# A chunked recurrence's block products moved from 128x128 to 64x64 tiles of the TensorE array

## The chip, the cores and the metric

The kernel runs on one core of one Trainium2 chip, as one program. The metric is device time in microseconds (us), the median of several runs. TensorE (PE) multiplies, and its weight loads are listed as an engine of their own (PEld). VectorE is DVE, ScalarE is ACT, GpSimd is POOL, and SyncE (SP) issues the DMAs.

## The reference, cut to what matters

The program computes two model blocks one after the other. The change lies in one mixer of the second block, a delta-rule recurrence over 512 tokens with 16 heads of width 64:

```python
def rwkv7_step(S, inp):
    r_t, dec_t, k_t, v_t, kk_t, a_t = inp
    sa = jnp.einsum('bhij,bhj->bhi', S, -kk_t)
    S = (S * dec_t[:, :, None, :]
         + sa[..., None] * (kk_t * a_t)[:, :, None, :]
         + v_t[..., None] * k_t[:, :, None, :])
    y = jnp.einsum('bhij,bhj->bhi', S, r_t)
    return S, y
...
S0 = jnp.zeros((B, H, N, N), jnp.float32)
_, y = lax.scan(rwkv7_step, S0, seq)
```

The kernel doesn't step token by token. It cuts the 512 tokens into 8 chunks of 64, and inside a chunk it solves the delta rule with the inverse of a 64x64 unit lower triangular matrix I+N, one for each head and chunk.

## The kernel before, in words

Two heads make a pair: head j of a pair lies on partitions 64j to 64j+63 (`hs[j]`). There are eight pairs, and two pairs make a quad. The recurrence is worked off in eight steps g: quad g // 2, and of its eight chunks the four of half g % 2.

`unit` prepares the four chunks of one pair for one g. It computes the inner products of the operands BK and AR (L1571), masks them with DVE into N, ME and RB, and inverts I+N. In bf16 it doubles the size of the inverted blocks over five levels: each level is a product z, a masked copy of it into Z by DVE (L1613), and the products T and Tt, which ACT copies out of PSUM (`keep`, L1606). Two refinements in float32 follow. All of these products come from `prod`: four matmuls, one for each chunk, each 128x128, with the two heads of a pair as the two 64x64 blocks on the diagonal of a 128x128 tile and zeros beside them. `turned` transposes four such tiles (L1601), and L1589 and L1638 transpose operands. `units` runs the generators of the two pairs of a quad step by step in turn.

`chain` is the serial part: 32 times (8 g with 4 chunks) it takes both pairs from the state of one chunk to that of the next. A chunk goes over gp (L1670), G (ACT, L1672), up (L1674), UV (ACT, two copies), xp (L1682) and the next XV (DVE, L1684), and adds two products per head to the output y: from XV (L1694) and from UV (L1695).

The main loop alternates one stage of `chain`, at a raised priority, with two steps of the units in flight (`advance`; STEPS = 24 steps for the 12 stages of a g). A scheduler then orders the instructions of each engine, and each engine runs its own in that order. A float32 product whose operands are not marked fp32r is one instruction in the program and two matmul passes in the trace; a bf16, an fp32r or a transposing one is one pass. Products in bf16 stand in the program as two instructions, LDWEIGHTS and MATMUL.

Before the first chain chunk the V projection (`values`, L366 to L368) fills PE; at the end the output projection does (`output_begin`, L1761).

Of the kernel before, what the change touches and what calls it, by code (L numbers as in the profile page):

```python
# [19 lines left out]
P = 128  # L20
# [1438 lines left out]
def rwkv_core(k, scr, filler, vstack, xsp):  # L1459
# [6 lines left out]
    with ExitStack() as s1, ExitStack() as s2:  # L1466
# [9 lines left out]
        NZ = 4  # L1476
        N_ = [cp.tile([P, 4, P], F32, name=f"N{i}") for i in range(NZ)]
        for n in N_:
            nc.vector.tensor_copy(n, c["ident"].unsqueeze(1).to_broadcast([P, 4, P]))
        Z_ = [[cp.tile([P, 4, P], BF, name=f"Z{l}_{i}") for l in range(5)] for i in range(2)]  # L1480
        for i in range(2):
            for l in range(5):
                nc.gpsimd.tensor_copy(Z_[i][l], c["b_ident"].unsqueeze(1).to_broadcast([P, 4, P]))
        mrw = c["m_rw"]
        bid = c["b_ident"]
        ide = c["ident"]
        two_i = c["two_i"].unsqueeze(1).to_broadcast([P, 4, P])
        one_i = ide.unsqueeze(1).to_broadcast([P, 4, P])
# [60 lines left out]
        count = [0]  # L1549
# [5 lines left out]
        def unit(g, ops, pr):  # L1555

            hf = par = g % 2
            p, AR, BK, bo, pl = ops
            N, Z = N_[count[0] % NZ], Z_[count[0] % 2]
            count[0] += 1  # L1560
            ME = held(g % 3).tile([P, 2, 4, P], F32, name="ME")
            RB = held(g % 3).tile([64, 2, 4, 64], F32, name="RB")
# [4 lines left out]
            for j in range(2):  # L1567
                a = psum()
                for u in range(4):
                    ch = 4 * hf + u  # L1570
                    nc.tensor.matmul(a[:, u], BK[hs[j], ch].rearrange("p a b -> p (a b)"),  # L1571
                                     AR[hs[j], ch].rearrange("p a b -> p (a b)"), start=True, stop=True)
                nc.sync.dma_start(ME[0:64, j], AR[hs[j], 4 * hf:4 * hf + 4].rearrange("p c a b -> p c (a b)"))
                nc.vector.copy_predicated(N[hs[j], :, hs[j]],
                                          mrw[0:64, 0:64].bitcast(I32).unsqueeze(1).to_broadcast([64, 4, 64]),
                                          a[0:64, :, 0:64])
                nc.vector.tensor_tensor(ME[64:P, j], a[64:P], mrw[64:P].unsqueeze(1).to_broadcast([64, 4, P]), op=ALU.mult)
                nc.vector.tensor_tensor(RB[:, j], a[0:64, :, 64:], mrw[0:64, 64:].unsqueeze(1).to_broadcast([64, 4, 64]), op=ALU.mult)
            yield
            Nb = tp.tile([P, 4, P], BF, name=f"Nb{par}")  # L1580
            nc.vector.tensor_scalar(Nb, N, -1.0, None, op0=ALU.mult)

            half = BK[:, 4 * hf:4 * hf + 4]
            nc.gpsimd.tensor_tensor(half.rearrange("p c a b -> p c (a b)"), half.rearrange("p c a b -> p c (a b)"),
                                    pl[:, 4 * hf:4 * hf + 4].unsqueeze(2).to_broadcast([P, 4, P]), op=ALU.mult)
            BT = held(g % 3).tile([P, 4, P], F32, name="BT")
            ps = psum()
            for u in range(4):
                nc.tensor.transpose(ps[:, u], BK[:, 4 * hf + u].rearrange("p a b -> p (a b)"), ide)  # L1589
            nc.scalar.copy(BT, ps)  # L1590
            def prod(lhs, rhs):
                o = psum()
                for u in range(4):
                    nc.tensor.matmul(o[:, u], lhs[:, u] if len(lhs.shape) == 3 else lhs,  # L1594
                                     rhs[:, u] if len(rhs.shape) == 3 else rhs, start=True, stop=True)
                return o

            def turned(t):
                o = psum()
                for u in range(4):  # L1600
                    nc.tensor.transpose(o[:, u], t[:, u].bitcast(F32), ide)  # L1601
                return o

            def keep(o, dt=F32R):
                t = tp.tile([P, 4, P], dt, name=("qr" if dt != BF else "qb") + str(par), bufs=4)
                nc.scalar.copy(t, o)  # L1606
                return t

            T, Tt = bid, bid
            for l in range(5):  # L1610
                yield
                z = prod(Nb, T)
                nc.vector.copy_predicated(Z[l], c[f"lv{l}"].bitcast(I16).unsqueeze(1).to_broadcast([P, 4, P]), z)  # L1613
                yield
                if l == 0:
                    T = Z[0]
                else:
                    T = keep(prod(Tt, Z[l]), F32R if l == 4 else BF)
# [3 lines left out]
            yield  # L1622
            z = prod(N, T.bitcast(F32))
            Z5 = tp.tile([P, 4, P], F32R, name=f"qr{par}", bufs=4)
            nc.vector.tensor_tensor(Z5, two_i, z, op=ALU.subtract)
# [4 lines left out]
            z = prod(N, T.bitcast(F32))  # L1630
            E = tp.tile([P, 4, P], F32R, name=f"qr{par}", bufs=4)
# [277 lines left out]
```

## Time and profile before

| | us |
|---|---|
| median of 3 runs (2564.41 to 2565.99) | 2565.23 |
| the profiled execution | 2561.08 |
| its span, first to last instruction | 2558.9 |
| PE busy in the span | 2437.7 |
| DVE busy | 1544.6 |
| ACT busy | 1096.5 |

The span lies 2.2 us below the time of its own execution, and that lies 4.1 us below the median. A matmul's entry as busy runs to the end of its pipeline, so that PE counts as busy in short gaps between matmuls; how densely matmuls follow each other is read from the length of a run of equal ones. The recurrence lies between about 980 and 1360 us of the span.

### The profile page before, as it was taken

The numbers are of one execution on the slowest core, as the hardware profiler recorded it, in microseconds if no ns is written. First come the engines' busy times: TensorE is split into PE (matmuls) and PEld (weight loads), VectorE is DVE, ScalarE is ACT, GpSimd is POOL, SyncE is SP. The second block draws the span as 40 slices with busy tenths as digits, with TensorE's granted clock in tenths as the row PEclk, the third lists the DMA queues.
The fourth block names the chain that finished last, engine by engine and source line by source line (L and its number), as shares of the span: only waits on it lengthen the run. The fifth ranks groups of instructions, "written<-read, shape, count | busy, mean of one in ns | idle before, by whom it ended". The sixth has DMA issues, their size and how long they took to land.

```text
span 2558.9 us, 32838 instructions
## 1 busy us (share of the span) xinstructions
PE 2437.7 (95%) x13114; PEld 1954.6 (76%) x13114; DVE 1544.6 (60%) x2194; ACT 1096.5 (43%) x1762; POOL 244.5 (10%) x222
## 2 busy tenths in 40 slices
PE   6999999999997999999999899999999798999997
PEld 5777777888886777788877688888865587888886
DVE  5345665633445877777547566565789665656555
ACT  5464544422323444666544443232432443423333
POOL 1001000000000564433101000000000100000000
PEclk8999999999998999999999999999999899999999
DMA  5112335122223335221143122222244131222221
GB/s 174 62 55 77 132 115 180 66 96 99 99 99 132 124 137 205 83 60 54 43 147 138 54 86 95 99 99 99 97 149 137 41 116 50 99 99 99 99 88 61
DMA packets 79126, 258.55 MB, mean 101 GB/s; under 512 B 10361, under 2 KB 21881, under 8 KB 61177
## 3 DMA queue, kind: packets, MB, share of 16 engines
q1 hardware_dynamic: 78972, 256.45, 29.8%
q8 instruction: 103, 1.69, 0.3%
q14 instruction: 51, 0.41, 0.0%
HBM read 217.94 MB, written 25.43 MB: 95 GB/s over the span
## 4 chain that ended last, share of the span: by engine, by line
PE 87%; DVE 5%; DMA 3%; ACT 3%; issue 2%; POOL 0%; SPq 0%; DVEq 0%; ACTq 0%; POOLq 0%
PE ps L366 21%; PE ps L367 21%; PE ps L368 20%; PE pt L1594 3%; PE ps L1203 1%; DVE wlo L331 1%; PE y L1695 1%; PE fl L366 1%; DMA raw<-xkv 1%; PE fl L367 1%; ACT whi L330 1%; PE fl L368 1%; PE pt L1571 1%; PE y L1694 1%; PE o L783 1%
## 5 line engine op out<-in xcount | busy, mean ns | idle before, releaser
L330 ACT CAST whi<-raw 128x2048 fp32r<-128x2048 f32 (+4 forms) x251 | 346.4, 1386 | 567.1 <-PE ps L368 450.8
L331 DVE TENSOR_TENSOR wlo<-raw,whi 128x2048 fp32r<-128x2048 f32 (+4 forms) x238 | 396.7, 1672 | 197.1 <-ACT whi L330 193.0
L937 DVE TENSOR_TENSOR x<-ps,x 128x512 f32<-128x512 f32 x94 | 64.1, 690 | 218.8 <-PE ps L368 218.8
L1127 ACT ACTIVATE cv<-u,vecs 128x512 f32<-128x512 f32 x88 | 63.0, 721 | 150.3 <-DVE u L1125 150.1
L1125 DVE TENSOR_TENSOR u<-ps,rms 128x512 f32<-128x512 f32 x88 | 60.3, 689 | 76.1 <-PE ps L368 76.0
L331 POOL TENSOR_TENSOR wlo<-raw,whi 128x512 fp32r<-128x512 f32 (+2 forms) x13 | 32.1, 2477 | 600.9 <-ACT whi L330 600.9
L1333 POOL TENSOR_SCALAR mx<-h,vecs 128x512 f32<-128x512 f32 x40 | 81.2, 2035 | 62.3 <-DVE mx6l L358 28.1
L1606 ACT CAST qb<-pt 128x512 bf16<-128x512 f32 x112 | 63.8, 590 | 36.1 <-PE pt L1594 35.3
L1128 DVE SCALAR_TENSOR_TENSOR cv<-u,vecs,cv 128x512 f32<-128x512 f32 x88 | 65.7, 749 | 11.2 <-ACT cv L1127 10.9
L366 PE MATMUL ps<-xg0h,wlo 128*128 128x512 f32 x164 | 68.3, 419 | 0.0
L1129 DVE SCALAR_TENSOR_TENSOR cv<-u,vecs,cv 128x512 f32<-128x512 f32 x88 | 65.8, 749 | 1.7
L367 PE MATMUL ps<-xg0l,whi 128*128 128x512 f32 x164 | 64.4, 393 | 1.0 <-DVE xg0l L361 1.0
L1613 DVE CAST_PREDICATED Z<-ball,pt 128x512 bf16<-128x512 int16 x80 | 53.1, 683 | 20.2 <-PE pt L1594 19.7
L367 PE MATMUL ps<-xg6l,whi 128*128 128x512 f32 x164 | 64.0, 390 | 1.1 <-DVE xg6l L361 1.1
L367 PE MATMUL ps<-xg7l,whi 128*128 128x512 f32 x164 | 63.9, 390 | 0.5 <-DVE xg7l L361 0.5
L368 PE MATMUL ps<-xg0h,whi 128*128 128x512 f32 x164 | 64.3, 392 | 0.0
L366 PE MATMUL ps<-xg1h,wlo 128*128 128x512 f32 x164 | 64.2, 392 | 0.0
L367 PE MATMUL ps<-xg1l,whi 128*128 128x512 f32 x164 | 64.2, 392 | 0.0
L368 PE MATMUL ps<-xg1h,whi 128*128 128x512 f32 x164 | 64.2, 392 | 0.0
L366 PE MATMUL ps<-xg2h,wlo 128*128 128x512 f32 x164 | 64.1, 392 | 0.0
L368 PE MATMUL ps<-xg7h,whi 128*128 128x512 f32 x164 | 64.0, 390 | 0.0
L368 PE MATMUL ps<-xg3h,whi 128*128 128x512 f32 x164 | 64.0, 390 | 0.0
(1239 smaller groups left out, 7150.5 us busy)
## 6 DMA issues: line engine op xcount, KB each, us to landing
raw<-ffn_in SPq DMA_DIRECT2D x44, 1024.0 KB, 4.8
raw<-xkv SPq DMA_DIRECT2D x64, 256.0 KB, 3.0
raw<-w_up SPq DMA_DIRECT2D x16, 1024.0 KB, 4.8
raw<-w_down SPq DMA_DIRECT2D x16, 1024.0 KB, 4.7
raw<-ffn_out SPq DMA_DIRECT2D x16, 1024.0 KB, 4.7
rk_scr<-ev SPq DMA_DIRECT2D x48, 256.0 KB, 2.1
ut<-ub SPq DMA_DIRECT2D x128, 67.5 KB, 2.0
raw<-w_in_fm SPq DMA_DIRECT2D x16, 512.0 KB, 3.9
```

Of the source, the lines that this page charges most:

```text
L330: a = hi_on.tensor_copy(hi[:, m], raw) if hi_on else nc.scalar.copy(hi[:, m], raw)
L331: b = (lo_on or nc.vector).tensor_tensor(lo[:, m], raw, hi[:, m].bitcast(F32), op=ALU.subtract)
L366: nc.tensor.matmul(ps, wl, xh, start=start, stop=False, skip_group_check=skip)
L367: nc.tensor.matmul(ps, wh, xl, start=False, stop=False, skip_group_check=skip)
L368: nc.tensor.matmul(ps, wh, xh, start=False, stop=stop, skip_group_check=skip)
L937: nc.vector.tensor_tensor(k.x[i], ps, k.x[i], op=ALU.add)
L1127: nc.scalar.activation(t, u[:, 2:], AF.Copy, scale=d(2))
L1128: nc.vector.scalar_tensor_tensor(t, u[:, 1:S + 1], d(1), t, op0=ALU.mult, op1=ALU.add)
L1129: nc.vector.scalar_tensor_tensor(t, u[:, 0:S], d(0), t, op0=ALU.mult, op1=ALU.add)
L1333: nc.gpsimd.tensor_scalar(t, h[m][:, 0:S], k.v(f"mu{i}", m), None, op0=ALU.mult)
L1594: nc.tensor.matmul(o[:, u], lhs[:, u] if len(lhs.shape) == 3 else lhs, rhs[:, u] if len(rhs.shape) == 3 else rhs, start=True, stop=True)
L1606: nc.scalar.copy(t, o)
```

## The change

Two pairs now share a tile: `unit` handles both pairs of a quad at once, in tiles of shape [128, 2, 4, 64] (pair, chunk, column), with head 0 of each pair on partitions 0 to 63 and head 1 below. No zeros are stored beside the blocks. `prod` issues 16 matmuls of 64x64 instead of four of 128x128 for each pair, with the two heads in turn, which uses two of the four 64x64 tiles of the array: rows 0 to 63 with columns 0 to 63, and rows 64 to 127 with columns 64 to 127. Both write the same PSUM tile, on its two halves of partitions. The inner products use all four 64x64 tiles (x and y). `turned` and the operand transposes become float32 products with a 64x64 identity (`token_major`), and the fp32r tiles become float32. In `chain`, up is split by head, and the product of XV with ME for the output moves ahead to stand right behind gp.

```diff
-        N_ = [cp.tile([P, 4, P], F32, name=f"N{i}") for i in range(NZ)]
-        Z_ = [[cp.tile([P, 4, P], BF, name=f"Z{l}_{i}") for l in range(5)] for i in range(2)]
+        N_ = [cp.tile([P, 2, 4, 64], F32, name=f"N{i}") for i in range(2)]
+        Z_ = [[cp.tile([P, 2, 4, 64], BF, name=f"Z{l}_{i}") for l in range(5)] for i in range(2)]
...
-            for j in range(2):
-                a = psum()
+            for i, (p, AR, BK, bo, pl) in enumerate(both):
...
+                x, y = psum(), psum()
                 for u in range(4):
                     ch = 4 * hf + u
-                    nc.tensor.matmul(a[:, u], BK[hs[j], ch].rearrange("p a b -> p (a b)"),
-                                     AR[hs[j], ch].rearrange("p a b -> p (a b)"), start=True, stop=True)
...
+                    for o, cols, kind in ((x, (0, 1), 0), (y, (1, 0), 1)):
+                        for j in range(2):
+                            nc.tensor.matmul(o[hs[cols[j]], u], BK[hs[j], ch, kind],
+                                             AR[hs[j], ch].rearrange("p a b -> p (a b)"), start=True, stop=True)
...
             def prod(lhs, rhs):
-                o = psum()
-                for u in range(4):
-                    nc.tensor.matmul(o[:, u], lhs[:, u] if len(lhs.shape) == 3 else lhs,
-                                     rhs[:, u] if len(rhs.shape) == 3 else rhs, start=True, stop=True)
+                o = eight(psum())
+                for i in range(2):
+                    for u in range(4):
+                        for r in hs:
+                            nc.tensor.matmul(o[r, i, u], lhs[r, i, u], rhs[r, i, u] if len(rhs.shape) == 4 else rhs[r],
+                                             start=True, stop=True)
                 return o
...
             def turned(t):
-                o = psum()
-                for u in range(4):
-                    nc.tensor.transpose(o[:, u], t[:, u].bitcast(F32), ide)
-                return o
...
+                return prod(t, idc)
...
+            def token_major(src, cols, put):
+
+                os = [eight(psum()) for _ in range(2)]
+                for i in range(2):
+                    for u in range(4):
+                        for j in range(2):
+                            for n, q in enumerate(cols):
+                                nc.tensor.matmul(os[j][hs[q], i, u], src(i, u, n)[hs[j]], idc[hs[j]], start=True, stop=True)
+                for j in range(2):
+                    put(j, os[j])
...
         def chain(hf, us, UV, XV, XN, PL, yps):
...
+                out = lambda pr, j: yps[pr][hs[j], ch * 64:ch * 64 + 64]
+                for pr in range(2):
+                    for j in range(2):
+                        nc.tensor.matmul(out(pr, j), XV[:, u, j, pr], MEs[pr][:, j, u, 64:], start=True, stop=False)
                 G = hA.tile([P, 2, 64], F32, name="G")
                 yield i, nc.scalar.mul(G, gp, -1.0)
                 for pr in range(2):
-                    i = nc.tensor.matmul(up[:, pr], us[pr][3][:, u], G[:, pr], start=True, stop=True)
+                    for j in range(2):
+                        i = nc.tensor.matmul(up[hs[j], pr], T2t[hs[j], pr, u], G[hs[j], pr], start=True, stop=True)
...
                 for pr in range(2):
-                    ME, RB, _, _ = us[pr]
                     for j in range(2):
-                        o = yps[pr][hs[j], ch * 64:ch * 64 + 64]
-                        nc.tensor.matmul(o, XV[:, u, j, pr], ME[:, j, u, 64:], start=True, stop=False)
-                        i = nc.tensor.matmul(o, UV[0:64, u, j, pr], RB[:, j, u], start=False, stop=True)
+                        i = nc.tensor.matmul(out(pr, j), UV[0:64, u, j, pr], RBs[pr][:, j, u], start=False, stop=True)
```

How this moves the instructions on PE is seen at two places; a row is line, operation, written tile, read tiles (moving operand's tile and the weights' tile, in either order), shape of the output, and how many follow each other. The first is the output part of a chunk in `chain`. Before, the products with UV (L1695) and with ME and XV (L1694) take turns, and the next chunk's gp (L1670) comes in between:

```order
L1571 MATMUL pt_11075<-AR,BK 128x128 x4
L1695 MATMUL y<-RB,UV 64x64
L1694 MATMUL y<-ME,XV 64x64
L1695 MATMUL y<-RB,UV 64x64 x2
L1670 MATMUL pc<-XV,ME 64x64
L1694 MATMUL y<-ME,XV 64x64
L1670 MATMUL pc<-XV,ME 64x64
L1695 MATMUL y<-RB,UV 64x64
```

Now gp is L1685, the product with ME and XV is L1689, up is L1694, xp is L1702 and the product with UV is L1712; L1612 is `prod`, L1631 `token_major`, and L1727 and L1733 belong to `post`:

```order
L1685 MATMUL pc<-XV,ME 64x64 x4
L1689 MATMUL y<-ME,XV 64x64 x4
L1631 MATMUL pt_13116<-idc,vv 64x64 x8
L1727 MATMUL ps<-y,call 128x512
L1694 MATMUL pc<-G,T2t 64x64 x4
L1631 MATMUL pt_13117<-idc,vv 64x64 x8
L1612 MATMUL pt_13138<-qr_13084,qr_13103 64x64 x9
L1712 MATMUL y<-RB,UV 64x64
L1702 MATMUL pc<-UV,BT 64x64 x4
L1712 MATMUL y<-RB,UV 64x64 x3
L1612 MATMUL pt_13138<-qr_13084,qr_13103 64x64 x7
```

The four products of a kind now stand together; over the recurrence the places where PE goes from one tile size to another fall from 350 to 222. The second place is in the middle of a unit. Before, PE alternates between the pairs, four matmuls each:

```order
L1594 LDWEIGHTS Nb_11114
L1594 MATMUL pt_11182<-Z_1_7980,Nb_11114 128x128
L1670 MATMUL pc<-XV,ME 64x64
L1694 MATMUL y<-ME,XV 64x64 x2
L1601 MATMUL pt_10902<-r_ident,qr_10877 128x128 x4
L1594 MATMUL pt_10909<-qr_10870,N_7969 128x128 x4
```

Now 16 pairs of LDWEIGHTS and MATMUL of one product (the last pair of one and the first of the next are shown) stand between two stages of the chain:

```order
L1612 LDWEIGHTS Z_1_7995
L1612 MATMUL pt_12797<-qb_12747,Z_1_7995 64x64
L1702 MATMUL pc<-UV,BT 64x64 x4
L1712 MATMUL y<-RB,UV 64x64 x4
L1612 LDWEIGHTS Nb_12674
L1612 MATMUL pt_12827<-qb_12795,Nb_12674 64x64
```

Over the recurrence the bf16 products go from 832 to 1664 and the float32 passes of the units (float32, fp32r and transposes) from 864 to 2816; DVE's masked copies into Z go from 80 to 40, and ACT's copies at `keep` from 176 to 88, each of the same 128x512 elements.

## Rows read from the trace of the kernel before

**Rows 1.** The page's first part: busy us of each engine, share of span, instructions.

```profile
PE 2437.7 (95%) x13114; PEld 1954.6 (76%) x13114; DVE 1544.6 (60%) x2194; ACT 1096.5 (43%) x1762; POOL 244.5 (10%) x222
```

**Rows 2.** Busy time in the stretches of the recurrence, all engines.

```profile
core 0: us, PE busy (x) PEld busy (x) DVE busy (x) ACT busy (x) POOL busy (x), PEclk, DMA share, GB/s
980.00:1016.00 36.00, 32.65 (x140) 24.58 (x138) 26.04 (x42) 14.86 (x22) 5.82 (x12) 0.91 0.59 206
1016.00:1066.00 50.00, 43.65 (x373) 35.15 (x372) 39.12 (x64) 33.87 (x64) 21.15 (x21) 0.97 0.44 136
1066.00:1300.00 234.00, 230.81 (x2361) 191.70 (x2359) 160.13 (x284) 144.67 (x322) 64.36 (x81) 1.00 0.18 51
1300.00:1322.00 22.00, 20.38 (x150) 15.82 (x149) 9.03 (x14) 9.19 (x19) 0.79 (x2) 0.77 0.68 258
```

**Rows 3.** The chain that ended last, by line, 1066 to 1300 us.

```profile
by line: PE pt L1594 32.9%; PE y L1695 10.6%; PE pt L1571 9.7%; PE y L1694 8.5%; PE pt L1601 5.7%; PE pc L1674 4.8%; PE pc L1670 4.6%; PE pc L1682 4.5%; PE pt L1589 2.8%; PE ps L1710 2.6%; PE ps L1716 2.4%; PE ps L1544 1.6%; ACT qb L1606 1.
```

**Rows 4.** The instructions of line L1670 (gp), with first and last start.

```profile
L1670 PE MATMUL pc<-XV,ME x256: 222/222/367, 1066.2 to 1321.8; 128*64 128x64 f32 x128
```

**Rows 5.** PE groups by line, 980 to 1335 us: passes, busy us, mean ns.

```profile
L1695 PE MATMUL y<-RB,UV 64*64 64x64 f32 x256 | 37.1, 243 | 1.6 <-ACT UV L1676 1.6
L1694 PE MATMUL y<-ME,XV 128*64 128x64 f32 x256 | 35.9, 238 | 0.0
L1594 PE MATMUL pt<-qr,N 128*128 128x128 f32 x256 | 35.7, 283 | 0.3 <-ACT qr L1606 0.3
L1571 PE MATMUL pt<-AR,BK 64*128 64x128 f32 x256 | 33.3, 285 | 0.4 <-DVE RB L1578 0.2
L1594 PE MATMUL pt<-Z,qb 128*128 128x128 bf16 x256 | 24.9, 221 | 3.3 <-DVE Z L1613 2.5 <-ACT qb L1606 0.5
L1594 PE MATMUL pt<-qr,qr 128*128 128x128 f32 x128 | 21.5, 290 | 0.5 <-ACT UV L1641 0.4
L1674 PE MATMUL pc<-G,T2t 128*128 128x64 f32 x128 | 19.7, 277 | 0.6 <-ACT G L1672 0.6
L1601 PE MATMUL pt<-r_ident,qr 128*128 128x128 f32 x128 | 19.6, 277 | 0.0
L1589 PE MATMUL pt<-r_ident,BK 128*128 128x128 f32 x64 | 10.1, 280 | 0.8 <-DVE RB L1578 0.4 <-ACT BT L1590 0.2
```

**Rows 6.** PE's timeline at 1168 us: start, length of the run, matmuls.

```profile
1168.04 0.61 PE L1594 MATMUL pt<-qb,Nb 128*128 128x128 bf16 x8
1168.58 0.33 PE L1695 MATMUL y<-RB,UV 64*64 64x64 f32 x2
1168.83 0.33 PE L1694 MATMUL y<-ME,XV 128*64 128x64 f32 x2
1169.09 0.33 PE L1695 MATMUL y<-RB,UV 64*64 64x64 f32 x2
...
1169.46 0.57 PE L1682 MATMUL pc<-UV,BT 128*64 128x64 f32 x7
1169.96 0.44 PE L1695 MATMUL y<-RB,UV 64*64 64x64 f32 x4
```

**Rows 7.** The same view at 1173 and at 1202 us.

```profile
1173.14 0.46 PE L1670 MATMUL pc<-XV,ME 128*64 128x64 f32 x8 [0.23 <-issue]
...
1202.07 0.33 PE L1695 MATMUL y<-RB,UV 64*64 64x64 f32 x4
```

**Rows 8.** The same view at 1181 and at 1206 us.

```profile
1181.28 2.00 PE L1594 MATMUL pt<-qr,N 128*128 128x128 f32 x16
...
1205.99 1.71 PE L1571 MATMUL pt<-AR,BK 64*128 64x128 f32 x16
```

**Rows 9.** DVE and ACT groups by line, 980 to 1335 us, as rows 5.

```profile
L1613 DVE CAST_PREDICATED Z<-ball,pt 128x512 bf16<-128x512 int16 x80 | 53.1, 683 | 20.2 <-PE pt L1594 19.7
...
L1606 ACT CAST qb<-pt 128x512 bf16<-128x512 f32 x112 | 63.8, 590 | 36.1 <-PE pt L1594 35.3
L1606 ACT CAST qr<-pt 128x512 fp32r<-128x512 f32 x64 | 36.5, 590 | 19.5 <-PE pt L1594 11.1 <-PE pt L1601 8.0
```

More of the change, by code (lines that the diff above doesn't have):

```diff
@@ L1553, in held, with unit @@
             return later["h"] if i else hA
-        def unit(g, ops, pr):
+        def unit(g, both):
             hf = par = g % 2
[L1558 to L1562, printed above, removed]
+            N, Z = N_[par], Z_[par]
+            hb = 1 if g % 3 == 0 else 2
+            BT = held(g % 3).tile([P, 2, 4, P], F32, name="BT", bufs=hb)
+            MEs, RBs = [], []
@@ L1596, in prod, with keep @@
                 return o
             def turned(t):
-                o = psum()
-                for u in range(4):
-                    nc.tensor.transpose(o[:, u], t[:, u].bitcast(F32), ide)
-                return o
-            def keep(o, dt=F32R):
-                t = tp.tile([P, 4, P], dt, name=("qr" if dt != BF else "qb") + str(par), bufs=4)
+                return prod(t, idc)
+            def keep(o, dt=F32):
+                t = tp.tile([P, 2, 4, 64], dt, name=("qr" if dt != BF else "qb") + str(par), bufs=4)
@@ L1610, in unit @@
+            T, Tt = None, bic
             for l in range(5):
-                yield
-                z = prod(Nb, T)
-                nc.vector.copy_predicated(Z[l], c[f"lv{l}"].bitcast(I16).unsqueeze(1).to_broadcast([P, 4, P]), z)
+                z = prod(Nb, T if l else bic)
+                nc.vector.copy_predicated(flat(Z[l]), over(lvc[:, l].bitcast(I16)), flat(z))
                 yield
@@ L1616, in unit @@
                     T = Z[0]
+                    token_major(lambda i, u, n: both[i][2][:, 4 * hf + u, n], (0, 1),
+                                lambda j, o: nc.scalar.copy(BT[:, :, :, hs[j]], o))
                 else:
-                    T = keep(prod(Tt, Z[l]), F32R if l == 4 else BF)
+                    T = keep(prod(Tt, Z[l]), F32 if l == 4 else BF)
                 if l == 4:
@@ L1621, in unit @@
                 Tt = keep(turned(T)) if l == 4 else keep(prod(Z[l], Tt), BF)
[L1622 to L1625, printed above, removed]
+                yield
+            z = prod(N, T)
+            Z5 = tp.tile([P, 2, 4, 64], F32, name=f"qr{par}", bufs=4)
+            nc.vector.tensor_tensor(flat(Z5), over(twc), flat(z), op=ALU.subtract)
             yield
@@ L1629, in unit, with place @@
             Tt = keep(turned(T))
[L1630 to L1632 removed]
+            z = prod(N, T)
+            E = tp.tile([P, 2, 4, 64], F32, name=f"qr{par}", bufs=4)
+            nc.vector.tensor_tensor(flat(E), over(idc), flat(z), op=ALU.subtract)
             yield
             UV, XV = values(g)
[L1635 to L1642 removed]
+            vvs = [value(b[0], b[3]) for b in both]
+            def place(j, o):
+                nc.scalar.copy(UV[64:P, :, j], o[64:P].rearrange("p r u d -> p u r d"))
+                nc.gpsimd.tensor_copy(XV[64:P, :, j], UV[64:P, :, j])
+            token_major(lambda i, u, n: vvs[i][:, hf * 256 + u * 64:hf * 256 + u * 64 + 64], (1,), place)
             yield
             z = prod(E, Tt)
[L1645 to L1659 removed]
+            T2t = held(g % 2).tile([P, 2, 4, 64], F32, name="T2t", bufs=1)
+            nc.vector.tensor_tensor(T2t, z, Tt, op=ALU.add)
+            return MEs, RBs, BT, T2t
         def chain(hf, us, UV, XV, XN, PL, yps):
             nonlocal SP
+            MEs, RBs, BT, T2t = us
             for u in range(4):
@@ L1817, in begin @@
                 aside()
-            running.append((g, units(*[(g, quads[g // 2][1][i], i) for i in range(2)])))
+            running.append((g, unit(g, quads[g // 2][1])))
             if g % 2 and g < KT - 1:
```

86 lines of the change are left out of this document (36 added, 50 removed).

## The prediction

> **What bounds the kernel now.** The page gives the whole first: PE is busy in 95% of the span, DVE in 60%, ACT in 43% [rows 1]. That is an average over many stages, so I read the stretches of the recurrence next [rows 2]. From 1066 to 1300 us PE is busy for 230.8 of 234 us, DVE for 160, ACT for 145, at a granted clock of 1.00, which is 2.4 GHz. Before that, from 1016 to 1066, PE is busy for 43.7 of 50 us and DVE for 39; from 1300 on the chain ends and the output projection begins. The chain that ended last goes almost only over PE lines of the units (L1594, L1571, L1601, L1589) and of the chain (L1670 to L1695), and an ACT copy has 1.6% [rows 3]. So PE's own queue sets the pace. The first and last gp show it from the other side: 32 chunks start within 255.6 us [rows 4], 8.2 us for each of the 31 steps.
>
> A busy PE may still be a badly packed one. A run of n equal passes lasts n-1 starts and one pass from its start to its end, so its length gives the time from start to start. Eight bf16 passes with 128 weight columns take 0.61 us, one takes 0.22: (0.61 - 0.22) / 7 = 0.056 us [rows 5, 6]. Sixteen float32 passes on 128 columns: (2.00 - 0.28) / 15 = 0.115 [rows 5, 8]. Float32 passes with 64 columns that stay on one tile: (0.57 - 0.222) / 6 = 0.058 [rows 4, 6]. With 64 columns that alternate between the two column halves of the array (gp): (0.46 - 0.222) / 7 = 0.034, and four 64x64 passes that alternate take 0.33 us where four mostly on one tile take 0.44 [rows 4, 6, 7]: two tiles work at once, and a long run should come near half of 0.058, 0.029. I take **0.030** for 64-column passes that alternate. Two row halves at once show only at the inner products, which write different PSUM tiles: 16 passes in 1.71 us, (1.71 - 0.285) / 15 = 0.095 against 0.115 [rows 5, 8], a partial overlap where j goes from 0 to 1.
>
> Going from one tile size to another has a price. L1695 (64 rows) and L1694 (128 rows) start 0.255 us apart with two passes each [rows 6]; two passes should take 0.116, so a change costs 0.14 us.
>
> **The change, part by part** (passes counted in the order, prices as above, us over the whole recurrence).
>
> Chain. *up*: 128 passes x 0.115 = 14.7 become 256 x 0.030 = 7.7, so -7.0. *Output*: 512 passes x 0.058 = 29.7. The half with ME now alternates, 256 x 0.030 = 7.7; the half with RB keeps its tile from one to the next about every second time, 256 x 0.044 = 11.3; together -10.7. *Changes of tile size*: 350 become 222, 128 x 0.14 = -17.9. gp and xp are as before. Sum of the chain: **-35.6**.
>
> Units. *bf16*: 832 x 0.056 = 46.6 become 1664 x 0.030 = 49.9, +3.3. Half the zeros are gone, but a pass does a quarter of the array and twice as many are needed. *Float32 products, fp32r and transposes*: (256 + 128 + 128) x 0.115 = 58.9 become 1536 x 0.030 = 46.1, -12.8. *Inner products*: 256 x 0.095 = 24.3. The new ones have 64 weight columns but stream 128 columns, for which there is no row; 512 passes cost between 512 x 0.115 / 4 = 14.7 (four tiles at once) and 512 x 0.115 / 2 = 29.4 (two). I take 20, nearer to four, since x and y are separate PSUM tiles: -4. *Transposes of operands*: 96 x 0.115 = 11.0 become 768 x 0.030 = 23.0, +12. Sum of the units: **-1.5**.
>
> PE in all: -37. DVE and ACT lose half of the Z copies, 40 x 0.683 = 27.3 us, and half of `keep`, 88 x 0.59 = 51.9 us [rows 9]. Between 1066 and 1300 neither engine is the bound, so I cost this at nothing there; PE's 230.8 busy us are its cover. From 1016 to 1066 DVE is nearly as busy as PE [rows 2], and fewer copies there should give some **-3**.
>
> What is late next: a unit is now one generator, where it was two taking turns. While DVE masks z (0.68 us) the next product of the unit can't start, and the other pair's four matmuls no longer stand in the gap. What can stand there is a stage of the chain: eight passes, 0.24, and two changes of tile size, 0.28. The copy and the run-out of the product take 0.68 + 0.22, so 0.4 us stay open. A unit has 17 steps, eight units 136; where a second unit is in flight its product of 0.48 us fills the gap. If half of the steps stand alone: 68 x 0.4 = 27 us. Some of them are filled by post, prep and the inner products of the next unit. Bounds 0 and 30; I take **+13**, the middle of what would be open.
>
> Sum: -37 - 3 + 13 = **-27**. Against the profiled execution, 2561.1 - 27 = 2534; with the 4.1 us by which the median lies above it, **2538 us**.
>
> The step that everything hangs on is that two tiles with different rows overlap. 4224 passes of the new kernel (1664 + 1536 + 256 + 768) are priced at 0.030; with 27 us in hand the change loses from 0.030 + 27 / 4224 = 0.036 on. No row shows two row halves that write the same PSUM tile at once. The Trainium skill ("TensorEngine Tiling (Array Packing)", Restrictions and Gotchas, Gotcha 1) says that different row tiles can't access the same PSUM bank at the same time, which `prod` now does with every neighbour; no run here shows it, and by it the first rival below would be the forecast.
>
> **The rivals.**
>
> 1. *The two row halves take turns, because they write one PSUM tile.* For it: nothing in the trace overlaps in this way, and the overlap of the inner products, in different PSUM tiles, is short [rows 8]. Against: the halves of the output lie on different partitions, and column halves of one PSUM tile (gp, L1695) do overlap [rows 7]. Then the bf16 products cost 1664 x 0.058 = 96.5 (+49.9), float32 1536 x 0.058 = 89.1 (+30.2), up 14.8 (+0.1), inner products 29.4 (+5), transposes, which write one PSUM tile for each row half, still +12; with -10.7 and -17.9 and -3 that is +66: 2561 + 66 + 4 = **2631 us**, slower. This decides from 0.036 us per pass on.
>
> 2. *bf16 pairs don't go faster than they do now.* Each is two instructions, LDWEIGHTS and MATMUL, and none in the trace follows closer than 0.056 us [rows 6]; float32 needs one instruction for two passes. If it is the issue that holds them, 1664 x 0.056 = 93.2, +43 against the sum. PE is then bound by these, and I count only 2 us of gaps: -37 - 3 + 43 + 2 = +5, **2570 us**. Against: with 128 columns a pass at 0.056 is also simply the time to stream them.
>
> 3. *The gaps eat the gain.* One unit alone leaves 0.4 us at each of its steps, and nothing else is ready: with 27 to 35 us of gaps the kernel stays at **2555 to 2565 us**. For it: twice the work per step and half the streams. Against: before, each unit's Z copies queue up behind each other on DVE, and now there are half of them.
>
> 4. *More is won.* If a bf16 pass with 64 streamed columns takes half of 0.056 on its tile, two tiles reach 0.015: 1664 x 0.015 = 25, -25 more, **2513 us**. Nothing in the trace has 64 bf16 columns. The Trainium skill ("TensorE: Matmul & The Clock Gate", LDWEIGHTS and the weight-path modes) says that fast weight loading needs 128 columns and that a plain load takes its number of columns divided by 1.2 in ns, an estimated 0.053 us here; by it this rival would fall away and the sum would stay.
>
> **How the numbers follow.** Forecast 0.53 (its own range 2520 to 2554: gaps of 0 to 30, inner products at either bound), rival 1 0.12, rival 2 0.13, rival 3 0.12, rival 4 0.10. The predicted time is that of the forecast. The range leaves out rival 1 and the far ends of the others: 2504 to 2584, some 0.83. A change of 0.2%, 5 us, is about what a measurement of this kernel can tell from none. Faster by more: the forecast, rival 4, and 0.05 of rival 3, 0.68. Within it: 0.05 of rival 3 and 0.03 of rival 2, 0.08. Slower: rival 1, the rest of rival 2, 0.02 of rival 3, 0.24.
>
> **What would show it.** Right: 16 float32 products of `prod` (32 passes) take about 0.96 us and a last pass, 16 bf16 pairs about 0.48; chunks of the chain 7.3 to 7.6 us apart; PE with visible idle time before L1612 that ends with the Z copy; DVE with 40 Z copies. Wrong: 32 passes in 1.85 us (rival 1), bf16 pairs at 0.056 (rival 2), idle time of PE above 30 us (rival 3). I would also be wrong if a change of tile size cost more than 0.14 us between 64x64 and 128x64 tiles, of which the new order has 138, or if PE's waits lowered the granted clock, as where it waited after 1300 us, at a mean of 0.77 [rows 2].

## The result, and the profile after

The changed kernel takes 2584.26 us, the median of four runs (2583.08 to 2587.02), beside 2565.56 for the kernel before (four runs, 2564.41 to 2565.99): a ratio of 1.0075, with a 95% interval of 1.0058 to 1.0093. It is slower by 0.75%, and the prediction of 2538 us was wrong. The profiled execution of the changed kernel took 2583.08 us.

First the page's part 1 of the changed kernel, then its windows (columns as in the rows of before):

```profile
PE 2411.9 (93%) x16026; PEld 1932.0 (75%) x16026; DVE 1496.5 (58%) x2110; ACT 1048.9 (41%) x1658; POOL 238.4 (9%) x216
```

```profile
1016.00:1066.00 50.00, 37.13 (x631) 27.43 (x630) 27.73 (x47) 17.45 (x31) 18.29 (x19) 0.87 0.38 118
1066.00:1300.00 234.00, 198.09 (x4800) 168.55 (x4802) 121.28 (x205) 107.61 (x235) 59.62 (x66) 0.89 0.17 51
1300.00:1322.00 22.00, 16.73 (x212) 12.69 (x209) 14.04 (x21) 10.83 (x23) 4.04 (x4) 0.79 0.71 261
```

Every engine has less to do [rows 1]. But from 1016 to 1322 us PE is idle for 54.1 of 306 us (306 - 37.1 - 198.1 - 16.7), where it was for 11.2 [rows 2]: **+43 us**. And the granted clock is down: busy time multiplied by what the clock lacks of 1.00 gives 37.1 x 0.13 + 198.1 x 0.11 + 16.7 x 0.21 = 30.1 us, where it was 6.0 [rows 2]: **+24 us**. This is an estimate: it takes a busy microsecond at half clock for half a microsecond of work. PE's busy time over the whole kernel fell by 25.8 us, although some 24 us of what is left are paid to the clock, so that its work at full clock fell by an estimated **50 us**. +43 + 24 - 50 = +17, most of the 22.3 us between the two spans; the rest lies outside these windows. The sum is no test of the 24, which stands in it twice, once in the 50: what was measured is 43 us more of idle time and 25.8 us less of busy time.

The instructions of gp, and the chain that ended last from 1016 to 1092 us, by line:

```profile
L1685 PE MATMUL pc<-XV,ME x256: 222/222/369, 1089.6 to 1339.1; 128*64 128x64 f32 x128
```

```profile
by line: DMA pg<-rk_scr 23.6%; PE pt L1612 7.1%; PE pt L1631 7.1%; issue 5.8%; DVE ME L1597 5.5%; POOL kk L1525 3.9%; POOL BK L1529 3.3%; POOL q L1528 3.3%; DVE RB L1598 3.0%; PE y L368 3.0%; PE y L366 2.8%; PE y L367 2.7%; DVE Z L1638 2.6%
```

The 32 chunks need 249.5 us instead of 255.6, 8.0 us for each step, not 7.3 to 7.6, but the first starts 23.4 us later [rows 4]. The largest share before it belongs to no part of a unit: it is the load of pg, with which `prep` begins. `prep` makes a pair's operands AR and BK in a chain over seven operations on ACT, six on DVE and, from pair 2 on, six on POOL (five without the product of r, as the expectations below count them); pg has two buffers, so a pair's load starts when the pair two before it has written its BK.

What that does to a unit, in the timeline of the changed kernel (SPq is the DMA queue of SP):

```profile
1135.42 0.33 SPq L1505 DMA_DIRECT2D pg<-rk_scr  x1
...
1140.58 0.49 DVE L1532 TENSOR_SCALAR q<-pg,vecs 128x512 f32<-128x512 f32 x1 [3.15 <-DMA pg<-rk_scr]
1140.98 0.68 DVE L1522 TENSOR_SCALAR q<-ps 128x512 f32<-128x512 f32 x1
1141.58 0.68 DVE L1533 SCALAR_TENSOR_TENSOR q<-q,pg 128x512 f32<-128x512 f32 x1
...
1142.18 0.68 DVE L1638 CAST_PREDICATED Z<-lvc,pt 128x512 bf16<-128x512 int16 x1
...
1142.91 0.64 PE L1612 MATMUL pt<-Z,qb 64*64 64x64 bf16 x16 [4.97 <-DVE Z L1638]
```

The mask Z, for which PE waits 4.97 us, isn't late because DVE is busy. DVE stands for 3.15 us at L1532, an operation of the preparation of a later quad, until its pg has landed 5 us after the issue; Z is queued behind it. ACT does the same; its waits from 1016 to 1330 us (total, times, longest):

```profile
ACT kk L1515 <- POOL q L1528: 13.2, 4, 4.4
ACT e L1508 <- DMA pg<-rk_scr: 12.2, 4, 4.1
...
ACT q_t L412 <- DVE q L1522: 8.8, 4, 4.3
ACT q L1517 <- POOL BK L1529: 7.9, 3, 5.1
```

These four are all lines of the preparation, 42.1 us in which ACT copies nothing for a unit. In the kernel before, ACT waits at lines of the preparation in two places in the same window, for 6.6 us:

```profile
ACT e L1500 <- DMA pg<-rk_scr: 4.2, 1, 4.2
...
ACT kk L1507 <- POOL AR L1518: 2.4, 1, 2.4
```

Not all of this reaches PE. Of its 54 us of idle time, 18.0 us lie in five gaps of 2 us or more, of which the example is the longest; the kernel before has no gap that long. The windows around the example show what follows for the clock:

```profile
1138.00:1143.00 5.00, 0.09 (x5) 0.08 (x6) 2.28 (x4) 1.27 (x3) 1.55 (x2) 0.91 0.30 128
1143.00:1162.00 19.00, 13.77 (x264) 12.54 (x263) 7.33 (x13) 9.14 (x23) 6.01 (x10) 0.50 0.28 85
1162.00:1178.00 16.00, 16.00 (x399) 13.45 (x398) 6.92 (x13) 8.07 (x18) 2.26 (x3) 0.98 0.12 36
```

After 5 us in which PE was busy for 0.09, the granted clock is 0.50, the 1.2 GHz level, for 19 us, and 0.98 in the 16 us behind them, in which PE has no gap. The same product shows both levels (granted clock 0.50 from 1069 to 1072 us, 1.00 from 1105 to 1107):

```profile
1069.87 1.97 PE L1612 MATMUL pt<-qr,qr 64*64 64x64 f32 x32
...
1105.90 1.10 PE L1612 MATMUL pt<-qr,N 64*64 64x64 f32 x32
```

### The profile page after: what moved, and what is told of

Same layout as the page of the kernel before. It is cut to its first block, busy times and chain, and to the rows that moved or that the text cites. A ratio compares the mean times of both kernels' runs of the same rounds, so it can differ in the third digit from the quotient of the medians.

```text
span 2581.2 us, 38409 instructions
## 1 busy us (share of the span) xinstructions
PE 2411.9 (93%) x16026; PEld 1932.0 (75%) x16026; DVE 1496.5 (58%) x2110; ACT 1048.9 (41%) x1658; POOL 238.4 (9%) x216
## 3 DMA queue, kind: packets, MB, share of 16 engines
q1 hardware_dynamic: 78972, 256.45, 29.2%
## 4 chain that ended last, share of the span: by engine, by line
PE 82%; DVE 5%; DMA 5%; ACT 4%; issue 2%; POOL 1%; SPq 0%; DVEq 0%; ACTq 0%; POOLq 0%
PE ps L366 21%; PE ps L367 20%; PE ps L368 20%; PE pt L1612 2%; DMA pg<-rk_scr 2%; PE ps L1203 1%; PE fl L366 1%; PE fl L367 1%; PE fl L368 1%; DMA raw<-xkv 1%; ACT whi L330 1%; PE pt L1631 1%; DVE wlo L331 1%; PE o L783 1%; PE s L710 1%
## 5 line engine op out<-in xcount | busy, mean ns | idle before, releaser
L1128 DVE SCALAR_TENSOR_TENSOR cv<-u,vecs,cv 128x512 f32<-128x512 f32 x88 | 65.7, 748 | 11.2 <-ACT cv L1127 10.9
L367 PE MATMUL ps<-xg2l,whi 128*128 128x512 f32 x164 | 64.4, 393 | 0.0
L368 PE MATMUL ps<-xg2h,whi 128*128 128x512 f32 x164 | 64.3, 392 | 0.0
L366 PE MATMUL ps<-xg6h,wlo 128*128 128x512 f32 x164 | 64.0, 390 | 0.0
```

The source lines that it names most:

```text
L366: nc.tensor.matmul(ps, wl, xh, start=start, stop=False, skip_group_check=skip)
L367: nc.tensor.matmul(ps, wh, xl, start=False, stop=False, skip_group_check=skip)
L368: nc.tensor.matmul(ps, wh, xh, start=False, stop=stop, skip_group_check=skip)
L1128: nc.vector.scalar_tensor_tensor(t, u[:, 1:S + 1], d(1), t, op0=ALU.mult, op1=ALU.add)
```

## The experiments

My first theory (A) was that gaps ate the gain, since a unit is now one stream whose copies also stand behind the preparation. Its rivals: the chain's regrouping loses (B), the 64x64 tiles or slow copies lose (C, D), the clock loses (E). Ratios are to the kernel before, timed on the same chip, with 95% intervals; the changed kernel itself has 1.0075.

**The two halves of the change.** The first run is the kernel before with the chain's part alone; the second the changed kernel with the output's products back in one place:

```diff
-                    i = nc.tensor.matmul(up[:, pr], us[pr][3][:, u], G[:, pr], start=True, stop=True)
+                    for j in range(2):
+                        i = nc.tensor.matmul(up[hs[j], pr], us[pr][3][hs[j], u, hs[j]], G[hs[j], pr], start=True, stop=True)
```

```diff
-                for pr in range(2):
-                    for j in range(2):
-                        nc.tensor.matmul(out(pr, j), XV[:, u, j, pr], MEs[pr][:, j, u, 64:], start=True, stop=False)
...
+                        nc.tensor.matmul(o, XV[:, u, j, pr], MEs[pr][:, j, u, 64:], start=True, stop=False)
                         i = nc.tensor.matmul(out(pr, j), UV[0:64, u, j, pr], RBs[pr][:, j, u], start=False, stop=True)
```

> The kernel before with the chain's part of the change alone (products with ME for the output right behind gp, up split by head), units as before. Theory A (the time of the change went into gaps of PE, because a unit is one stream that waits on copies, and these copies stand behind the preparation of the next quad on ACT and DVE; the chain's regrouping is a gain): two pairs still take turns, PE stays filled, and most of the 36 us of the sum shows: 2535 us, 2525 to 2545. Rival B (the regrouping itself loses, or a change of tile size costs nothing, so that there is nothing to win): 2560 us or more.

> The changed kernel with the output's products at the end of a chunk again, interleaved as before; units and the split of up as changed. Theory A: the units' part alone is a loss, since its gaps stay and the chain's gain goes: 2600 us, 2590 to 2610, less than the full 29 us more than 2584 because part of the extra PE work falls into gaps. Rival B (the regrouping is what loses): 2575 us or less.

Measured: 2554.26 us, 0.9962 (0.9949 to 0.9974), and 2591.82 us, 1.0108 (1.0094 to 1.0122). The regrouping is a gain, which rules out B, but here of 10 us, not 36. The pages of the two runs:

```profile
PE 2424.0 (95%) x13242; PEld 1941.8 (76%) x13242; DVE 1542.4 (60%) x2194; ACT 1097.4 (43%) x1762; POOL 246.3 (10%) x222
```

```profile
PE 2433.3 (94%) x16026; PEld 1944.5 (75%) x16026; DVE 1496.0 (58%) x2110; ACT 1050.8 (41%) x1658; POOL 239.8 (9%) x216
```

PE's busy time fell by 13.7 us in the first [rows 1]. That is no measure of the whole term of -35.6, because with the units on 128x128 tiles most changes of tile size stay: counted over the recurrence, the first run's trace has 311, where the kernel before has 350 and the changed kernel 222. 39 changes at 0.14 us and the -17.7 of up and output make -23. The second run takes the output's part out of the changed kernel: it has 330 changes, 108 more, and PE is busy for 21.4 us more, where 108 x 0.14 and the output's 10.7 make 25.8. So the 0.14 us came out somewhat high in both, but not by much. The first version is faster than both kernels, and the fastest here that leaves nothing out.

**Unit 0 earlier, and two streams.** The next two attack the gaps directly: two steps of unit 0 at each step of the value projection (`advance(2)`), and the changed tiles with one generator per pair, as before:

```diff
-            running.append((g, unit(g, quads[g // 2][1])))
+            running.append((g, units(g, quads[g // 2][1])))
...
-                t = tp.tile([P, 2, 4, 64], dt, name=("qr" if dt != BF else "qb") + str(par), bufs=4)
+                t = tp.tile([P, 4, 64], dt, name=("qr" if dt != BF else "qb") + str(par), bufs=8)
```

> The changed kernel with two steps of unit 0 instead of one at each step of the value projection, so that the unit is finished under the projection's matmuls. Theory A, of which the largest single piece is the stretch before the first chunk (first gp at 1089.6 us against 1066.2): the first gp comes 10 to 15 us earlier, 2571 us, 2565 to 2578. Rival C (the 64x64 tiles, or the lower granted clock over the whole recurrence, carry the loss): 2580 to 2588 us.

> The changed kernel with its 64x64 tiles and its chain, but each quad's two pairs as two streams that take turns again: every product, mask and copy is for one pair (256 columns instead of 512), so DVE and ACT issue twice as many. Theory A (one stream is what opens the gaps): PE idle time in the recurrence falls back to near that of the kernel before and PE's 25 us less of busy time show: 2545 us, 2530 to 2560. Rival C (the tiles themselves cost it, or DVE and ACT work is what is late): 2575 us or more.

Measured: 2591.92 us, 1.0117 (1.0099 to 1.0134), and 2595.55 us, 1.0134 (1.0113 to 1.0155). Both are misses for theory A as I had put it. In the first the first gp does come 11.4 us earlier (1078.2), but the 32 chunks then take 269.4 us. In the second, two streams leave PE as idle as one: busy for 197.93 of 234 us from 1066 to 1300, at a clock of 0.84, in an execution that took 2608.93 us, the longest of its five. Two streams also mean twice as many copies of half the size. One stream instead of two is not the cause by itself.

**The preparation, and the clock.** Four runs: each step of the preparation queued behind the stage of the chain that it follows; fill matmuls ahead of every product; and the preparation of quads 1 to 3 left out, in the changed kernel and in the one before:

```diff
+                with k.queued(i):
                     aside()
...
+                for _ in range(3):
+                    for r in hs:
+                        nc.tensor.matmul(o[r, 0], bic[r], lvc[r, 0:4].rearrange("p a b -> p (a b)"), start=True, stop=True)
...
         def operands(q):
+            if q:
+                quads[q] = quads[0]
+                return
```

> The changed kernel with each step of the preparation of the next quads (and of post) queued behind the stage of the chain that it follows in the program, on the engines of that stage, so that it is not issued ahead of the first chunk. Theory A (copies of a unit wait behind preparation that itself waits for its transfer): the first gp comes 5 to 15 us earlier than 1089.6, PE's idle time from 1016 to 1340 falls from 54 to 35 to 45 us, 2565 to 2575 us. Rival D (the preparation's place doesn't matter; the single unit's own copies are too slow for PE): 2580 to 2590 us, idle time as before.

> The changed kernel with three pairs of matmuls of 256 bf16 columns put ahead of every product of a unit, into the tile that the product then overwrites: some 0.3 us of PE work each, 144 times, 46 us in all, which can start while PE would wait for a copy. Rival E (the lower granted clock after the gaps is a large part of the loss): the time at the half level from 1016 to 1340 falls from 78 us to 30 or less, which gives back up to 25 us, and most of the fill lies in the 54 us of gaps: 2565 to 2585 us, no slower than without. Theory A alone (the gaps, not the clock): the clock is as before or gives back little, and the fill that isn't hidden costs 15 to 40 us: 2600 to 2625 us.

> The changed kernel without the preparation of quads 1 to 3: all units take the operands of quad 0, so that six of the eight loads of pg, their ACT, DVE and POOL work and the loads of vv are left out; units and chain do all their work. Theory A: PE's idle time from 1016 to 1340 falls from 54 us to 20 or less, the granted clock stays up, 2525 to 2540 us. Rival D (the units' own copies): idle time stays above 35 us, 2560 to 2575 us, the rest being PE's and the queues' own work of the preparation.

> The kernel before with the same left out, as the control: PE has only 11 us of idle time there and its share of the preparation is six times 2 us of matmuls, so that some 10 to 20 us go, 2545 to 2555 us, by either theory. If theory A holds, the changed kernel without preparation is the faster of the two by 10 us or more; by rival D it is not.

Measured, in this order: 2580.54 us, 1.0063 (1.0048 to 1.0078); 2617.99, 1.0211 (1.0195 to 1.0226); 2536.14, 0.9894 (0.9879 to 0.9908); 2553.52, 0.9963 (0.9951 to 0.9976). The last two settle where the loss is: without the preparation (and the loads of vv that go with it) the changed kernel is the faster by 0.7%, 17 us, about as much as it is slower with it. The preparation costs 46 us there (1.81% of 2565) and 9.5 us in the kernel before. A difference of two such ratios is uncertain by some 5 us, by their intervals. The windows of the two:

```profile
1016.00:1066.00 50.00, 42.41 (x1044) 37.19 (x1036) 26.30 (x45) 16.06 (x29) 6.43 (x7) 0.95 0.22 63
1066.00:1300.00 234.00, 211.48 (x4772) 175.33 (x4771) 113.36 (x197) 106.62 (x240) 27.65 (x30) 0.93 0.22 65
```

```profile
1016.00:1066.00 50.00, 46.99 (x416) 40.07 (x414) 31.91 (x55) 25.91 (x50) 4.59 (x7) 0.93 0.20 58
1066.00:1300.00 234.00, 229.28 (x2372) 193.85 (x2373) 145.69 (x264) 136.84 (x306) 29.95 (x46) 0.98 0.18 53
```

From 1016 to 1300 PE is idle for 30.1 us without the preparation and 48.8 with it; in the kernel before 7.7 and 9.5 [rows 2]. So 19 of the 39 us of idle time by which the changed kernel exceeds the one before there go with the preparation, and some 20 stay without it. The queue alone gave back next to nothing. In its trace the first gp comes earlier (1078.0), but the preparation now comes late for the units, and PE waits for it itself:

```profile
PE pt L1590 <- POOL BK L1529: 10.8, 4, 5.9
```

The fill is inconclusive for the clock: over the span the granted clock is 0.971 with it and 0.965 without, and it costs 34 us, so it doesn't say what the clock alone is worth. The time lies in the range that I had given for theory A alone.

**One remedy for the preparation at a time.** Its POOL part on DVE; the same, queued; that with a third pg buffer; the third pg buffer alone; queued with the third buffer:

```diff
-            eng = nc.gpsimd if p > 1 else nc.vector
+            eng = nc.vector
...
-            pg = pp.tile([P, 4, S], F32, name="pg")
+            pg = pp.tile([P, 4, S], F32, name="pg", bufs=3)
```

> The changed kernel with the products of the preparation on DVE for all pairs, where pairs 2 to 7 had them on POOL (six chains of five operations, 1.27 us each on POOL, about 0.69 us on DVE). Theory F (the serial chain of the preparation, above all its POOL part, is too slow now that PE needs less time for a unit): the preparation of a pair gets some 3 us shorter and no longer holds the pg buffers, PE's idle time from 1016 to 1340 falls from 54 us to about 40, 2560 to 2572 us. Rival G (DVE becomes what is late, since 30 more operations of 0.69 us stand ahead of the units' masks there): 2582 to 2595 us.

> The same and the preparation queued behind the chain, as in the run with the queue alone (2580.5 us, where PE waited 10.8 us for POOL's last write of BK). Theory F: these waits go or shrink to a third, 2560 to 2570 us. Rival G: 2580 us or more.

> The same as the run before this with a third buffer for pg, so that the load of the next pair can start before the one in use is done (room for it comes from Nb, with one buffer instead of two). Theory A (units' copies wait behind a preparation that waits for its transfer): a further 3 to 8 us, 2555 to 2565 us. If the transfer isn't what is waited for any more: no difference to the run before this.

> The changed kernel with the third buffer for pg alone (and one for Nb). Theory A in its first form (the transfer of pg, 5 us, ahead of which ACT and DVE stand): the waits of ACT and DVE for pg before the first chunk go, some 10 us, 2572 to 2578 us. Theory F (the preparation's own chain of operations): 2580 to 2587 us.

> The changed kernel with the real preparation behind the chain and a third pg buffer, POOL's part on POOL as it was. If the late load of pg is what holds POOL there (PE waited 10.8 us for POOL's write of BK): 2566 to 2575 us. If the preparation's steps are slow by themselves: 2577 to 2590 us.

Measured: 2583.21 us, 1.0067 (1.0050 to 1.0085); 2587.76, 1.0085 (1.0068 to 1.0101); 2590.50, 1.0097 (1.0082 to 1.0112); 2590.55, 1.0101 (1.0086 to 1.0116); 2581.84, 1.0064 (1.0041 to 1.0087). The three runs with a third pg buffer have one buffer for Nb instead of two, to make room. None gives anything back that can be told from the changed kernel, so the runs show neither POOL nor the transfer as the one thing that is late.

**Dependence, time, or waits.** Three runs take the preparation apart. In the first it is computed in full, but the units take quad 0's operands; in the second most of its operations on ACT and DVE are cut to 64 of 512 columns; in the third, run after these, its operations stay (but for some small copies on POOL), queued as before in the program, and read and write tiles that make them wait for nothing:

```diff
-            quads[q] = PL, ops
+            quads[q] = quads.get(0, (PL, ops))
...
-            nc.scalar.activation(e3, cs, AF.Exp, scale=DEC)
+            w = slice(0, 64 if p > 1 else S)
+            nc.scalar.activation(e3[:, w], cs[:, w], AF.Exp, scale=DEC)
...
+            act = lambda f, **kw: nc.scalar.activation(sa, src, f, **kw)
+            mul = lambda e, o: e.tensor_tensor(o, src, src, op=ALU.mult)
```

> The changed kernel with the whole preparation of pairs 2 to 7 still computed (loads of pg, ACT, DVE, POOL and its matmuls), but into a tile that nothing reads: the units take quad 0's operands, so that no unit waits for a preparation and no preparation for a unit. Left out as in the run without preparation: the values of quads 1 to 3 and their sums. Theory H (the preparation's operations, wherever they stand, are in the way of the units' copies on ACT and DVE): most of its 48 us stay, 2570 to 2585 us. Theory I (the two-way dependence, units for operands and preparation for free buffers, opens the gaps): 2540 to 2555 us.

> The changed kernel with the preparation of pairs 2 to 7 cut to 64 of 512 columns in its seven operations on ACT, five of its six on DVE, one of its five on POOL and its matmul, so that these take some 0.15 to 0.3 us instead of 0.6 to 0.7; order, loads, buffers and dependences stay. Theory H (time of these operations on ACT and DVE): 2550 to 2565 us. Theory I (the waits between the preparation's steps and for its buffers): 2572 to 2584 us.

> The changed kernel with the preparation behind the chain (the places of the run with the queue alone, 2580.5 us) and all its loads and operations for pairs 2 to 7, of the same engines, functions and sizes, but each reads one constant tile and writes one that nothing reads: no operation of it waits for a transfer, for POOL, for another of its steps or for a buffer, and no unit waits for it. Left out besides: the values of quads 1 to 3. Theory J (what costs is the preparation's waits for its own transfers and steps, since the unit's copies stand behind the waiting operation on ACT and DVE): 2540 to 2558 us, idle time near that of the run without preparation, 36 us. Theory H (the operations themselves are in the way): 2565 us or more.

Measured: 2579.21 us, 1.0055 (1.0039 to 1.0070); 2574.60, 1.0044 (1.0028 to 1.0061); 2551.92, 0.9952 (0.9935 to 0.9970). The first is close to the changed kernel, so the dependence by itself isn't it; the second gives back some 8 us, so the operations' own time is a small part. The timeline of the longest of its ten executions shows that the gap stays with the smaller operations (this one took 0.75 us, three times the 0.25 that most of its kind take there):

```profile
1138.67 0.75 DVE L1538 TENSOR_SCALAR q<-pg,vecs 128x64 f32<-128x64 f32 x1 [2.23 <-DMA pg<-rk_scr]
...
1139.59 0.68 DVE L1645 CAST_PREDICATED Z<-lvc,pt 128x512 bf16<-128x512 int16 x1
1140.33 0.64 PE L1619 MATMUL pt<-Z,qb 64*64 64x64 bf16 x16 [5.18 <-DVE Z L1645]
```

The third has most of the answer. Beside the run with the queue (1.0063), the operations that wait for nothing cost 1.1% less, 28 us of the 46. Three things besides the waits differ. It takes the dependence away, which without the queue was worth 5 us, while in the run with the queue PE waited 10.8 us for BK. POOL's part is done by 1064 us, where it ran on to 1217. And quad 1's operations on ACT run from 987 to 1005 us instead of 1006 to 1056. This last change is not where the time is won: the first gp comes at 1078.1 in the third and 1078.0 in the run with the queue, the last at 1310.6 and 1332.1, and between the two gp the operations of quads 2 and 3 on ACT begin within 8 us of the same places. Its windows:

```profile
1016.00:1066.00 50.00, 44.51 (x780) 34.03 (x780) 34.74 (x47) 14.99 (x25) 40.20 (x35) 1.00 0.64 209
1066.00:1300.00 234.00, 210.26 (x4984) 178.58 (x4978) 123.45 (x218) 119.53 (x260) 30.91 (x34) 0.92 0.18 52
```

PE's idle time is 29.2 us, that of the run without preparation (30.1), and the clock is at 1.00 from 1016 until 1066. So with the waits and the dependence gone, all the idle time of these windows that goes with the preparation is gone too; the two were not separated from each other at these places.

**Less work on PE where two streams remain.** The faster version of the first run, with only the float32 end of a unit on 64x64 tiles:

```diff
+                        nc.tensor.matmul(o[r, u], at(lhs, r, u), at(rhs, r, u), start=True, stop=True)
...
-            z = prod(N, T.bitcast(F32))
+            z = blocks(N, T)
```

> The kernel before with the chain regrouped (2554.3 us) and only the float32 end of a unit (the product of l = 4, both Newton steps, T2t) on 64x64 tiles, heads below one another in [128, 4, 64] tiles; two pairs still take turns as two streams, and the bf16 steps stay 128x128. PE loses some 20 us of work, ACT and DVE half of their columns in these steps, and the bf16 part goes on covering the rest. If what hurts the changed kernel is PE's lack of cover in the serial bf16 steps: 2538 to 2550 us, faster than both. If any work taken from PE only turns into gaps and half clock: 2554 us or more.

Measured: 2558.78 us, 0.9979 (0.9967 to 0.9990): no faster than without (0.9962). The run decides little, because PE lost no work in it: over the whole it is busy for 2424.7 us, and for 2424.0 in the run without. Its trace has 404 changes of tile size over the recurrence and that of the run without 311, and 93 changes at 0.14 us are 13 us, about what the float32 products were to save. Its first gp also comes 11.8 us later (1078.2).

## Why the prediction was wrong

- **Two row tiles overlap: right.** The step on which I let everything hang held. 32 float32 passes take 1.10 us (1105.90, above), (1.10 - 0.222) / 31 = 0.028 us each, for 0.030. They write one PSUM tile with both row halves, on different partitions, and rival 1 is out. The rule from the Trainium skill ("TensorEngine Tiling (Array Packing)", Gotcha 1) does not hold for these two tiles.
- **bf16: mis-sized, to the good.** The timeline of the changed kernel at full clock:

```profile
1037.02 0.44 PE L1612 MATMUL pt<-Z,Nb 64*64 64x64 bf16 x16
...
1082.69 0.19 PE L1612 MATMUL pt<-Z,qb 64*64 64x64 bf16 x1
```

  That is (0.44 - 0.19) / 15 = 0.017 us per pass, near rival 4's price; the term of +3.3 is some -18. The estimate of 0.053 us that the prediction worked out from the Trainium skill ("TensorE: Matmul & The Clock Gate", LDWEIGHTS and the weight-path modes) differs from this row, also if each of the two tiles is taken alone (0.033).
- **Inner products and transposes of operands: mis-sized, to the bad.** Three rows at full clock, or nearly:

```profile
1114.59 1.08 PE L1631 MATMUL pt<-idc,vv 64*64 64x64 f32 x15
...
1120.79 1.09 PE L1590 MATMUL pt<-AR,BK 64*64 64x128 f32 x16
...
1131.46 1.81 PE L1631 MATMUL pt<-idc,BK 64*64 64x64 f32 x64
```

  An inner product takes (1.09 - 0.27) / 15 = 0.055 us per pass, 28 us for 512 instead of the 20 that I took: two tiles at once, not nearly four. The transposes of BK take 0.025, but those of vv, whose two row halves write the same 64 partitions, (1.08 - 0.22) / 14 = 0.061, the price of one tile alone. Together that is some +21 where -4 and +12 were priced.
- **The chain: somewhat mis-sized.** In the changed kernel the output's part of the -35.6, priced at -28.6, measured 21.4 us of PE's busy time (the second run); up was not measured apart.
- **DVE and ACT: right.** DVE has 40 Z copies for 80 [rows 9], and PE's idle time ahead of `prod` ends most often with them, for 11.4 us of the 54; the groups of both, 980 to 1360 us:

```profile
L1638 DVE CAST_PREDICATED Z<-lvc,pt 128x512 bf16<-128x512 int16 x40 | 27.3, 685 | 22.7 <-PE pt L1612 22.2
```

```profile
L1612 PE MATMUL pt<-Z,qb 64*64 64x64 bf16 x512 | 17.3, 208 | 11.5 <-DVE Z L1638 11.4
```

- **PE's work in all** came out at an estimated -50 by busy time and clock; the terms as measured add up to some -40 (chain -28 with up as priced, bf16 -18, float32 -15, the other two +21), for my -37. That the terms meet the sum is luck: bf16 made up for the others. If PE had stayed the bound, the kernel would have been about as fast as forecast, or faster.
- **The failed step: "What is late next", +13.** I counted only the copy for which a unit waits itself, 0.4 us at half of its steps, with bounds 0 and 30. Without the preparation the copies alone come out in that range, if above the +13: 30.1 us of idle time against 7.7, some 22. What I put at nothing, without giving a reason, is what else stands in the queues of ACT and DVE; I named the preparation only as something that fills gaps. The same preparation ran in the kernel before, but ACT waited at its operations for 6.6 us there and waits for 42.1 now, so that its price could not be read off the trace of before; that the queues hold it could. It takes PE's idle time to +43 us. This is rival 3 with another mechanism and a higher price than its 27 to 35 us (which, by the sum of the prediction, make 2552 to 2560 us and not 2555 to 2565).
- **DVE's early stretch, -3: wrong in sign.** From 1016 to 1066 DVE did fall from 39 to 28 us, but the first chunk came 23.4 us later. Without the preparation of later quads it comes at 1058.3 us instead of 1089.6, so this too goes with the preparation.
- **The clock** was named among what would make me wrong, and got no price: +24 us, an estimate. That the fall follows the gaps is read from the windows; its share wasn't separated by an experiment.
- **A reading that changes nothing:** the 1.6% of [rows 3] belong to PE's L1544; the row breaks off in the share of the ACT copy, which stands behind it and is no larger.

What stays open: of the preparation's 46 us, some 28 are its waits (with the dependence), 3 its place, which is less than these ratios can tell from nothing, and 15 remain between the run that waits for nothing and the one without preparation. That these are the operations' time on ACT and DVE, and the later first chunk (1078.1 against 1058.3 us), was not taken apart further. Why the same operations wait so much longer than in the kernel before was not shown either.

## What to carry to other kernels

A busy PE is also a cover: before work is taken from it, ask for each engine that feeds it not only how busy it is, but what stands in its queue ahead of the copies, and for what that waits. Here operations of a later stage, which wait for a transfer or a slower engine, cost 9.5 us while PE had enough to do and 46 once it hadn't. Shortening them gave back some 8 us, and giving one of their waits room nothing that could be told from noise. And a gap on PE of some microseconds can be paid twice, as here at 1138 us: once as idle time and once as work at the lower clock after it. When tiles of two sizes are mixed, count the changes between them: at some 0.14 us each they ate what the last run was to save.

## What the runs showed of the hardware

Two 64x64 tiles with different rows and columns work at once on one PSUM tile: 0.028 us per float32 pass and 0.017 us per bf16 pass with 64 columns, where 128x128 passes took 0.115 and 0.056 [rows 5, 6, 8]. Two with different rows and the same columns took turns, though in different PSUM tiles: 0.061 us per float32 pass. At the granted clock of 0.50 the same run of 32 float32 passes takes 1.97 us instead of 1.10. After 5 us without work the clock stayed at this level for 19 us, in which PE was busy for 13.8.
